# Bias table written later, openings with their token sums and row inside the blocks, and the closing attention's fillers laid out anew

## The chip, the core and the metric

The kernel runs on one core of a Trainium2 chip, as one launch. The metric is the device time of that launch in microseconds (us). Before the change it is 2303.39 us, the median of three runs that lie between 2301.87 and 2303.82 us.

## The reference, cut to what matters

Two transformer blocks are computed one after the other for a sequence of T = 256 tokens, width D = 2048, all in float32.

```python
def first_block(x, c, ...):
    sh1, sc1, g1, sh2, sc2, g2 = split(silu(c) @ w_mod + b_mod, 6)
    h = rms_norm(x, norm_attn) * (1 + sc1) + sh1
    qa, ka, va, qb, ckv, qi, ki, wi = split(h @ w_in)
    out_a = swa_attention(qa, ka, va, attn_sinks, rel_a)       # window 128, bias by bucketed distance
    out_b = dsa_attention(qb, rms_norm(ckv), w_uk, w_uv, qi, ki, wi, rel_b)   # top-64 keys, bias too
    x = x + g1 * (concat(out_a, out_b) @ w_out)
    h = rms_norm(x, norm_ffn) * (1 + sc2) + sh2
    x = x + g2 * conv_ffn(h, w_up, conv_w, conv_b, w_down)
    return rms_norm(x, norm_final)

def second_block(x, c, ...):
    x = x + gA * gmlp_mixer(rms_norm(x) * (1 + scA) + shA, ...)
    k_nope, k_rope, v = mla_shared_kv(rms_norm(x, kv_norm) * (1 + kvsc) + kvsh, ...)
    x = x + gB * mla_mixer(rms_norm(x) * (1 + scB) + shB, k_nope, k_rope, v, ...)   # 16 heads, causal
```

The bias of both attentions of the first block comes from one table: `rel_bias` (32 buckets x 32 heads) spread over 384 distances.

## The kernel before, in words

**Products.** Every weight is streamed from memory once: SyncE's queue (SP) starts the loads, 1 MB each into one of five buffers `raw` (`load`, L323). ScalarE (ACT) rounds a half of a block to its high part `wh` (L331), VectorE (DVE) forms the rest `wl` (L332), each in five buffers, and TensorE (PE) forms the product from three matmuls for each 128 x 128 piece (L342 to L344): high x high, high x low, low x high. A block of 2048 x 128 weights is two halves of 8 pieces, 48 matmuls in all. The results stand in eight PSUM banks, taken in turn.

**Order.** The program is written out in Python in one order; a scheduler turns it into a fixed sequence for each engine at build time, by its own model of readiness, and an instruction that comes later in the program may stand ahead of an earlier one that it holds not to be ready. On the chip each engine's sequence, and SP's, is worked off as it stands: an instruction that waits holds up those behind it.

**Beside the products** run 200 reductions on DVE over 1 MB pieces of the modulation weights (`mod_part`, L453 and L456) and some matmuls for the same purpose (`mod_cols`, L469 to L480).

**First attention, k-tiles.** The input projection goes tile by tile over the 16 pieces of the contraction: `tile_of(k)` loads `w_a[k]` (808 KB) and adds 13 products of three matmuls (L737 to L739) to seven banks that stay in use for the whole loop. The loop runs over eight pairs q of such tiles; between them the columns of `sc1` for the next pair are formed with the one bank left. After pair q == 5 comes `tables`: it loads five small constants, multiplies `rel_bias` by a one-hot matrix (L704), adds the mask on DVE (L706), and writes the sum, 32 x 384 numbers, to DRAM (`bias`, L708, on SP). The attention reads it from there much later (`attend`).

**Openings.** The feed-forward part, the gMLP and the last mixer (`mla`) each begin with `opening`. RMS norm needs the sum of squares over all features, which is complete only when the last block of x is. So the first blocks are multiplied with unnormalized pieces `xg`, and `finish` scales their results by R afterwards. Meanwhile `token_sums` (two matmuls with a column of ones, L307, per tile of squares) give the sums, `rsqrt` takes some 12 small DVE instructions (L271 to L285), `diagonal` two more (L293), and `row` spreads the root over the partitions by a matmul (L299). After `row`, `modulated` forms the normalized pieces xs (L521, L529, L262, L263), which later blocks use. Before the change the sums stand after block 0, the row after block 1.

**Last mixer.** After the opening come four blocks `w_bin[0..3]` (the raw queries). Between them stand `norm_root(raw_c)` after block 0, `normed(raw_c)` (the normalized latent `ck`) after block 1, and `norm_root(kr)` after block 2. Then follow gate blocks (`gate`, 16 of them, 48 matmuls each), which are needed late and serve as fillers: `fill(n)` puts n of them where the program would otherwise have only short, dependent steps. Then the attention over eight pairs of heads g: `weights` (scores and softmax), the queries of the next pair, fillers, keys and values of the next four heads, transposes (`outputs`, L605), and products with the values. From g == 4 on the fillers are the eight blocks of the first half of the output projection.

Of the kernel before, what the change touches and what calls it, by code (L numbers as in the profile page):

```python
# [37 lines left out]

WOB = (0, 2)

NPRE, NMID, NF, NG = 3, 2, 6, 5

RP, RWA, RWB, RF, RG, RM = 1.8, 1.25, 1.25, 0.82, 0.5, 0.6

# [158 lines left out]
class Build:  # L203
# [159 lines left out]
    def opening(self, src, n, sums, roots, rest):  # L363

        w = [self.weights(src(i), DB, 0) for i in range(NPRE)]
        out = [self.multiplied(w[0], self.xg, 2)]
        diag = self.diagonal(roots(sums()))
        out += [self.multiplied(w[i], self.xg, 2) for i in range(1, NMID)]
        R = self.row(diag)
        out += [self.multiplied(w[i], self.xg, 2) for i in range(NMID, NPRE)]  # L370
        with self.tc.issue_after(self.chain):
            rest(0, R)
            for i in range(NPRE, n):
                out.append(self.block(src(i), self.xg, 0, 2))
                rest(i - 2, R)
        return out, R
# [317 lines left out]
    def tables(self, pool):  # L694
        nc = self.nc
        self.causal = pool.tile([P, 384], F32, name="causal")
        nc.sync.dma_start(self.causal, self.ap["causal"])
        self.sinks = pool.tile([P, 16], F32, name="sinks")
        nc.sync.dma_start(self.sinks, self.ap["sinks"].to_broadcast((P, 16)))
        onehot, bneg, rel = (self.tmp("pT", (32, n)) for n in (384, 384, 32))  # L700
        for t, n in ((onehot, "onehot"), (bneg, "bneg"), (rel, "rel_bias")):
            nc.sync.dma_start(t, self.ap[n])
        ps = self.bank()
        nc.tensor.matmul(ps[:32, :384], rel, onehot, start=True, stop=True)  # L704
        bt = self.tmp("pT", (32, 384))
        nc.vector.tensor_add(bt, ps[:32, :384], bneg)  # L706
        self.bias = self.dr.tile([32, 384], F32, name="bias")
        nc.sync.dma_start(self.bias, bt)  # L708

    def first_attention(self):  # L710
        nc, ap = self.nc, self.ap
        with self.tc.tile_pool(name="pa", bufs=1, reuse_waits="tile") as pool:
# [5 lines left out]
            def modulated(blocks):  # L718
                s = slice(blocks[0], blocks[-1] + 1)
                nc.vector.scalar_tensor_tensor(gain[:, s], self.mod_tile("sc1")[:, s], 1.0,  # L720
                                               self.vec("norm_attn", blocks[0], len(blocks)), op0=OP.add, op1=OP.mult)
                xs.extend(self.modulated(self.R, gain, self.mod_tile("sh1"), blocks))
# [3 lines left out]
            def tile_of(k):  # L726

                raw = self.load(ap["w_a"][k], WA)
                x = xs[k]
                hl = [self.parts(raw, 0, 1024), self.parts(raw, 1024, WA)]  # L730
                for i in (12, *range(12)):
                    h, l = hl[i // 8]
                    n = 80 if i == 12 else P
                    s = slice(i % 8 * P, i % 8 * P + n)
                    ps = sums[i // 2][:n, i % 2 * T:i % 2 * T + T]
                    mm = nc.tensor.matmul
                    mm(ps, h[:, s], x[:, :T], start=k == 0 and i % 2 == 0, stop=False)  # L737
                    mm(ps, h[:, s], x[:, LO:], start=False, stop=False)  # L738
                    mm(ps, l[:, s], x[:, :T], start=False, stop=k == DB - 1 and (i % 2 == 1 or i == 12))  # L739

            modulated(range(2))
            for q in range(8):
                if q < 7:
                    a = self.mod_cols("sc1", q + 1)
                    next(a)
                    self.mod_part("sh1", 2 * q + 2)
                tile_of(2 * q)
                if q < 7:
                    next(a)
                    next(a, None)  # L750
                    self.mod_part("sh1", 2 * q + 3)
                    modulated(range(2 * q + 2, 2 * q + 4))
                tile_of(2 * q + 1)
                if q == 5:
                    self.tables(pool)

            keys = self.pair()
            kiT = keys[:, 0]
# [343 lines left out]
    def mla(self):  # L1102
        nc, ap = self.nc, self.ap
        mm = nc.tensor.matmul
        rate = RM
        with self.tc.tile_pool(name="pm", bufs=1, reuse_waits="tile") as pool:
# [15 lines left out]
            raw_q = [two[i // 2][:, i % 2] for i in range(4)]  # L1122
            for i in range(4):
                self.evac(raw_q[i], self.block(ap["w_bin"][i], xs, rate)[:, :T])
                if i == 0:
                    root_c = self.norm_root(raw_c, 512)
                if i == 1:
                    ck = self.normed(raw_c, root_c, self.vec("kva", 0, 4))
                if i == 2:
                    root_k = self.norm_root([kr[:64]], 64)  # L1130

            zs = {}
# [7 lines left out]
            def fill(n):  # L1140
                for _ in range(n):
                    next(more, None)
# [25 lines left out]
            krT = pool.tile([P, T], F32, name="krT")  # L1168
            nc.vector.tensor_add(krT, t1, kn)

            cq = self.normed(raw_q, root_q, self.vec("gqa", 0, 4))
            cs = self.tmp("t", (P, 2, 64))
            nc.sync.dma_start(cs.rearrange("p a b -> p (a b)"), ap["cs"])
            g = self.tmp("t", (P, 64))
# [9 lines left out]
            def keys(c4):  # L1184

                banks = self.token_block([ap["w_ukv"][c4]], ck, 512, rate)
                rn = self.head_roots(lambda tb: banks[tb], 4, P)
                kk = self.wp.tile([P, 2, 4, P], F32, name="kk", tag="c_all", bufs=1)
                for tb in range(2):
                    nc.vector.tensor_mul(kk[:, tb], banks[tb].rearrange("p (a b) -> p a b", a=4),  # L1190
                                         rn[:, tb * 4:tb * 4 + 4].unsqueeze(2).to_broadcast([P, 4, P]))
                yield
                kT = [self.pair(), self.pair()]
                for tb in range(2):
                    ps = self.bank()
                    for h in range(4):
                        nc.tensor.transpose(ps[:, h * P:(h + 1) * P], kk[:, tb, h], self.ident)
                    for half in range(2):
                        nc.scalar.activation(kT[half][:, :, tb * P:(tb + 1) * P], _two(ps[:, half * T:half * T + T]),
                                             AF.Copy, scale=self.vec("gkn"))  # L1200
                yield kT

            def values(c4):
                banks = self.token_block([ap["w_ukv"][4 + c4]], ck, 512, rate)
                vv = [self.pair(), self.pair()]
                for tb in range(2):
                    for half in range(2):
                        self.evac(vv[half][:, tb], banks[tb][:, half * T:half * T + T])
                return vv
# [68 lines left out]
            def outputs(g, s, vv):  # L1278
                pTs = [self.transposed(s[:, r]) for r in range(2)]
                yield  # L1280
                ys = []
                for r in range(2):
                    ps = self.bank()[:, :T]
                    self.values(ps, pTs[r], vv[:, 0, r * P:(r + 1) * P], vv[:, 1, r * P:(r + 1) * P])
                    y = self.tmp()
                    nc.vector.tensor_mul(y, ps, zs[g][:, r])
                    ys.append(self.split(y))
                yield ys
# [8 lines left out]
            def projects():  # L1297
                for b2 in range(8):
                    project(0, b2, ys, gB)
                    yield  # L1300
# [6 lines left out]
            vv = values(0)  # L1307
            fill(1)
            kT = next(k1)
            q = next(q1)  # L1310
            for g in range(8):
                if g == 4:
                    more = projects()
                s = weights(*q, kT[g])
                o = outputs(g, s, vv[g])
                if g < 7:
                    q1 = queries(g + 1)
                    next(q1)
                fill(2 if g < 4 else 1)
                if g % 2 == 1 and g < 7:  # L1320
                    k1 = keys(g // 2 + 1)
                    next(k1)
                    vv += values(g // 2 + 1)
                else:
                    fill(1)
                next(o)
                if g < 4 or g == 5:
                    fill(1)
                if g < 7:
                    if g % 2 == 1:  # L1330
                        kT += next(k1)
                    q = next(q1)
                (ys if g < 4 else ys2).extend(next(o))
# [34 lines left out]
```

## Time and profile before

| what | value |
|---|---|
| median of three runs | 2303.39 us |
| the profiled execution's own time | 2303.12 us |
| its span, first to last instruction | 2301.4 us |
| TensorE busy | 2241.6 us, 97% of the span |
| VectorE busy | 1830.5 us, 80% |
| ScalarE busy | 1157.8 us, 50% |
| mean data rate | 274 GB/s |

The span is 1.7 us shorter than the execution's own time. TensorE's busy time overlaps from one matmul to the next, so 97% does not say that the array works at its peak; the time in which TensorE has nothing at all to run is the 59.8 us that are missing to the span, and the slow clock comes on top where it has been idle for a while.

### The profile page before, as it was taken

How to read it: one execution, taken by the hardware profiler on the slowest of the kernel's cores; microseconds unless marked ns; L12 is line 12 of the kernel's file. 1: busy time of each engine (PE TensorE's matmuls, PEld its weight loads, DVE VectorE, ACT ScalarE, POOL GpSimd, SP SyncE). 2: the span in 40 equal slices, each digit the busy share in tenths (PEclk: the TensorE clock that was granted, in tenths of full speed). 3: DMA queues.
4: the chain of work that ended last, by engine and by line, in shares of the span. 5: the costliest groups of instructions: out<-in, count | busy, mean ns of one | idle time of the engine just before them, and what ended most of it. 6: DMA issues, size and time to landing. Idle time of an engine off the chain costs nothing.

```text
span 2301.4 us, 43110 instructions
## 1 busy us (share of the span) xinstructions
PE 2241.6 (97%) x17710; PEld 2137.8 (93%) x17710; DVE 1830.5 (80%) x2996; ACT 1157.8 (50%) x1918; POOL 4.0 (0%) x8
## 2 busy tenths in 40 slices
PE   6889999999999999999999999999999999999999
PEld 4778889999999999999998889999999999899899
DVE  5768988998898898888798769777776568766784
ACT  2346675664354444444675444435344456555652
POOL 0000000000000000000000000000000000000000
PEclk9999999999999999999999999999999999999999
DMA  8988998898898999899677776887775555444442
GB/s 342 410 334 316 342 350 317 299 323 323 327 375 319 337 361 341 304 366 335 206 252 282 282 276 246 292 284 275 279 273 187 186 187 180 143 155 156 138 147 92
DMA packets 98199, 629.61 MB, mean 274 GB/s; under 512 B 10994, under 2 KB 18130, under 8 KB 30802
## 3 DMA queue, kind: packets, MB, share of 16 engines
q1 hardware_dynamic: 98002, 626.87, 74.5%
q8 instruction: 138, 2.26, 0.4%
q14 instruction: 59, 0.48, 0.1%
HBM read 624.68 MB, written 2.15 MB: 272 GB/s over the span
## 4 chain that ended last, share of the span: by engine, by line
PE 89%; DVE 5%; ACT 2%; DMA 2%; issue 1%; SPq 0%; DVEq 0%; ACTq 0%
PE bank L342 23%; PE bank L343 23%; PE bank L344 23%; PE bank L408 4%; PE bank L409 4%; PE bank L410 4%; DVE wl L332 2%; PE bank L739 1%; PE bank L737 1%; DVE mraw L456 1%; PE bank L738 1%; PE bank L469 1%; DMA mraw<-in_wmods_dram 1%; ACT wh L331 1%; PE bank L1054 1%
## 5 line engine op out<-in xcount | busy, mean ns | idle before, releaser
L342 PE MATMUL bank<-act,wh 128*128 128x256 f32 (+1 forms) x4800 | 1357.4, 283 | 6.2 <-ACT act L549 2.6
L343 PE MATMUL bank<-act,wh 128*128 128x256 f32 x4800 | 1352.1, 282 | 0.2
L344 PE MATMUL bank<-act,wl 128*128 128x256 f32 (+1 forms) x4800 | 1346.6, 281 | 2.3 <-DVE wl L332 2.3
L331 ACT ACTIVATE wh<-raw 128x1024 fp32r<-128x1024 f32 (+3 forms) x770 | 766.2, 1002 | 708.3 <-PE bank L343 489.4
L332 DVE TENSOR_TENSOR wl<-raw,wh 128x1024 fp32r<-128x1024 f32 (+3 forms) x770 | 879.1, 1151 | 208.4 <-ACT wh L331 201.7
L342 PEld LDWEIGHTS bank<-act,wh 128*128 128x128 f32 x4800 | 907.8, 189 | 13.8 <-issue 4.4
L344 PEld LDWEIGHTS bank<-act,wl 128*128 128x128 f32 x4800 | 906.2, 189 | 3.2 <-DVE wl L332 2.9
L343 PEld LDWEIGHTS bank<-act,wh 128*128 128x128 f32 x4800 | 906.7, 189 | 1.0 <-DVE act L263 0.7
L456 DVE CUSTOM_DVE_ANT_0 mraw<-mraw,c_all,k_vecs 128x2048 f32<-128x2048 f32 x200 | 469.3, 2347 | 67.4 <-DMA mraw<-in_wmods_dram 63.3
L408 PE MATMUL bank<-wh,act 128*128 128x512 f32 (+1 forms) x392 | 151.9, 387 | 0.0
L409 PE MATMUL bank<-wl,act 128*128 128x512 f32 (+1 forms) x392 | 151.2, 386 | 0.0
L410 PE MATMUL bank<-wh,act 128*128 128x512 f32 (+1 forms) x392 | 150.9, 385 | 0.0
L262 ACT ACTIVATE act<-t 128x256 fp32r<-128x256 f32 x166 | 66.2, 414 | 95.2 <-DVE t L951 47.7
L408 PEld LDWEIGHTS bank<-wh,act 128*128 128x128 f32 x392 | 73.6, 188 | 15.7 <-PE bank L1258 1.0
L410 PEld LDWEIGHTS bank<-wh,act 128*128 128x128 f32 x392 | 73.6, 188 | 15.2 <-issue 0.7
L409 PEld LDWEIGHTS bank<-wl,act 128*128 128x128 f32 x392 | 73.6, 188 | 14.9 <-issue 0.7
L263 DVE TENSOR_TENSOR act<-t,act 128x256 fp32r<-128x256 f32 x166 | 67.6, 424 | 17.1 <-ACT act L262 16.3
L737 PE MATMUL bank<-act,wh 128*128 128x256 f32 (+1 forms) x208 | 59.7, 301 | 11.7 <-ACT wh L331 11.6
L738 PE MATMUL bank<-act,wh 128*128 128x256 f32 (+1 forms) x208 | 58.3, 294 | 0.0
L739 PE MATMUL bank<-act,wl 128*128 128x256 f32 (+1 forms) x208 | 54.2, 299 | 3.8 <-DVE wl L332 3.8
L737 PEld LDWEIGHTS bank<-act,wh 128*128 128x128 f32 (+1 forms) x208 | 40.8, 198 | 16.4 <-ACT wh L331 14.8
L578 DVE SCALAR_TENSOR_TENSOR X<-bank,m_g,X 128x256 f32<-128x256 f32 x96 | 46.0, 481 | 6.8 <-PE bank L344 4.8
(236 smaller groups left out, 1368.0 us busy)
## 6 DMA issues: line engine op xcount, KB each, us to landing
mraw<-in_wmods_dram SPq DMA_DIRECT2D x200, 1024.0 KB, 6.9
raw<-in_w_up_dram SPq DMA_DIRECT2D x88, 1024.0 KB, 6.4
raw<-in_w_down_dram SPq DMA_DIRECT2D x64, 704.0 KB, 5.5
raw<-in_w_u_dram SPq DMA_DIRECT2D x32, 1024.0 KB, 5.2
raw<-in_w_v_dram SPq DMA_DIRECT2D x32, 1024.0 KB, 4.9
raw<-in_w_z_dram SPq DMA_DIRECT2D x32, 1024.0 KB, 4.9
raw<-in_w_ao_dram SPq DMA_DIRECT2D x32, 1024.0 KB, 5.0
raw<-in_w_cols_dram SPq DMA_DIRECT2D x24, 1024.0 KB, 7.9
```

The lines of the kernel that those rows point to most:

```text
L331: nc.scalar.activation(h[:, :n], raw[:, lo:hi], AF.Copy)
L332: nc.vector.tensor_sub(l[:, :n], raw[:, lo:hi], h[:, :n].bitcast(F32))
L342: mm(ps[:, :n], h[:, s], x[:, :n], start=first and k == 0, stop=False)
L343: mm(ps[:, :T], h[:, s], x[:, LO:], start=False, stop=False)
L344: mm(ps[:, :n], l[:, s], x[:, :n], start=False, stop=last and k == len(xs) - 1)
L408: mm(ps, xh, h[:, s], start=k == 0, stop=False)
L409: mm(ps, xh, l[:, s], start=False, stop=False)
L410: mm(ps, xl, h[:, s], start=False, stop=k == kt - 1)
L456: self.nc.vector.tensor_tensor_reduce(out=raw, in0=raw, in1=self.c_all, scale=1.0, scalar=self.vec("b_" + name, j), op0=OP.mult, op1=OP.ad ...
L737: mm(ps, h[:, s], x[:, :T], start=k == 0 and i % 2 == 0, stop=False)
L738: mm(ps, h[:, s], x[:, LO:], start=False, stop=False)
L739: mm(ps, l[:, s], x[:, :T], start=False, stop=k == DB - 1 and (i % 2 == 1 or i == 12))
```

## The change

It does the following. `tables` is called after pair q == 4 instead of q == 5 and no longer writes the table to DRAM; the new method `table_out` does that, after pair q == 6. `opening` puts the token sums, the root and its diagonal between the two halves of block 0, and the row between the two halves of block 1. In `mla` the two roots and the normalized latent move one block later each; one filler goes ahead of the normalized queries, one ahead of the transposed queries of the first pair; and g = 0, 1 and 2 get one filler instead of two behind `weights`.

```diff
-NPRE, NMID, NF, NG = 3, 2, 6, 5
+NPRE, NF, NG = 3, 6, 5
 
     def opening(self, src, n, sums, roots, rest):
 
         w = [self.weights(src(i), DB, 0) for i in range(NPRE)]
-        out = [self.multiplied(w[0], self.xg, 2)]
+        out = [self.bank() for _ in range(2)]
+        self.product(out[0], w[0][0], self.xg[:8], True, False, ext=2)
         diag = self.diagonal(roots(sums()))
-        out += [self.multiplied(w[i], self.xg, 2) for i in range(1, NMID)]
+        self.product(out[0], w[0][1], self.xg[8:], False, True, ext=2)
+        self.product(out[1], w[1][0], self.xg[:8], True, False, ext=2)
         R = self.row(diag)
-        out += [self.multiplied(w[i], self.xg, 2) for i in range(NMID, NPRE)]
+        self.product(out[1], w[1][1], self.xg[8:], False, True, ext=2)
+        out += [self.multiplied(w[i], self.xg, 2) for i in range(2, NPRE)]
         with self.tc.issue_after(self.chain):
...
         bt = self.tmp("pT", (32, 384))
         nc.vector.tensor_add(bt, ps[:32, :384], bneg)
+        return bt
+
+    def table_out(self, bt):
         self.bias = self.dr.tile([32, 384], F32, name="bias")
-        nc.sync.dma_start(self.bias, bt)
+        self.nc.sync.dma_start(self.bias, bt)
...
                 tile_of(2 * q + 1)
-                if q == 5:
-                    self.tables(pool)
+                if q == 4:
+                    bt = self.tables(pool)
+                if q == 6:
+                    self.table_out(bt)
...
             for i in range(4):
                 self.evac(raw_q[i], self.block(ap["w_bin"][i], xs, rate)[:, :T])
-                if i == 0:
+                if i == 1:
                     root_c = self.norm_root(raw_c, 512)
-                if i == 1:
+                if i == 2:
                     ck = self.normed(raw_c, root_c, self.vec("kva", 0, 4))
-                if i == 2:
+                if i == 3:
                     root_k = self.norm_root([kr[:64]], 64)
...
             nc.vector.tensor_add(krT, t1, kn)
 
+            fill(1)
             cq = self.normed(raw_q, root_q, self.vec("gqa", 0, 4))
...
             vv = values(0)
             fill(1)
             kT = next(k1)
+            fill(1)
             q = next(q1)
             for g in range(8):
...
                 if g < 7:
                     q1 = queries(g + 1)
                     next(q1)
-                fill(2 if g < 4 else 1)
+                fill(2 if g == 3 else 1)
```

## Rows read from the trace of the kernel before

**Rows 1.** Windows by stage: busy us and count per engine, granted clock, DMA share, GB/s.

```profile
421.00:1177.00 756.00, 751.22 (x6345) 750.55 (x6346) 665.33 (x851) 377.20 (x561) 1.59 (x2) 1.00 0.88 322
1177.00:1919.00 742.00, 741.96 (x5546) 707.34 (x5545) 556.42 (x744) 347.27 (x459) 2.16 (x2) 1.00 0.71 252
1919.00:2018.00 99.00, 92.21 (x685) 88.38 (x684) 79.07 (x220) 57.99 (x103) 0.00 (x0) 0.97 0.47 158
2018.00:2253.00 235.00, 230.60 (x1671) 214.48 (x1670) 173.47 (x530) 135.25 (x275) 0.00 (x0) 1.00 0.44 151
```

**Rows 2.** SP's queue in time: start us, us of issuing, transfer; k-tile stage.

```profile
2.96 0.43 SPq L697 DMA_DIRECT2D causal<-in_causal_dram  x1
...
99.88 0.33 SPq L323 DMA_DIRECT2D raw<-in_w_a_dram  x1
...
108.53 0.42 SPq L702 DMA_DIRECT2D pT<-in_rel_bias_dram  x1
...
118.31 0.33 SPq L708 DMA_DIRECT2D bias<-pT  x1
118.73 0.38 SPq L323 DMA_DIRECT2D raw<-in_w_a_dram  x1
```

**Rows 3.** SP's waits, 110 to 120 us: us in total, times, longest.

```profile
SPq L708 <- DVE pT L706: 8.1, 1, 8.1
```

**Rows 4.** Timeline of the k-tile stage: start, us, instruction, [idle before <- releaser].

```profile
100.31 0.61 PE L478 MATMUL bank<-ones,t 128*128 128x1 f32 x4 [0.49 <-ACT t L474]
...
114.39 0.61 PE L478 MATMUL bank<-ones,t 128*128 128x1 f32 x4 [0.49 <-ACT t L474]
...
126.04 0.58 PE L737 MATMUL bank<-act,wh 128*128 128x256 f32 x1 [3.98 <-ACT wh L331]
...
135.09 0.61 PE L478 MATMUL bank<-ones,t 128*128 128x1 f32 x4 [0.49 <-ACT t L474]
```

**Rows 5.** Windows of 2 us in the k-tile stage, columns as in rows 1.

```profile
118.00:120.00 2.00, 2.00 (x19) 2.00 (x19) 2.00 (x3) 0.00 (x0) 0.00 (x0) 1.00 0.31 50
...
126.00:128.00 2.00, 1.96 (x8) 1.84 (x9) 1.91 (x2) 0.57 (x1) 0.00 (x0) 0.50 1.00 420
```

**Rows 6.** Timeline of the three openings (feed-forward, gMLP, last mixer).

```profile
464.60 0.51 PE L342 MATMUL bank<-act,wh 128*128 128x256 f32 x2 [0.74 <-ACT act L262]
...
1180.29 0.42 DVE L317 TENSOR_TENSOR nacc<-nacc,t 128x256 f32<-128x256 f32 x1
...
1182.43 0.50 PE L307 MATMUL bank<-ones,ssacc 128*128 128x1 f32 x4
...
1954.06 0.38 PE L342 MATMUL bank<-act,wh 128*128 128x256 f32 x1 [0.55 <-ACT act L262]
...
1956.28 0.39 PE L342 MATMUL bank<-act,wh 128*128 128x256 f32 x1 [0.90 <-ACT act L262]
```

**Rows 7.** Timeline of the last mixer behind its opening.

```profile
1960.76 0.99 PE L307 MATMUL bank<-ones,nacc 128*128 128x1 f32 x4 [3.52 <-DVE nacc L317]
...
1981.80 0.47 DVE L293 TENSOR_SCALAR t<-k_ident,rs_y 128x128 f32<-128x128 f32 x2
...
1987.28 0.68 PE L299 MATMUL bank<-t,ones 128*128 128x256 f32 x2
...
1995.74 0.67 PE L299 MATMUL bank<-t,ones 128*128 128x256 f32 x2 [1.67 <-DVE t L293]
...
2020.52 0.49 PE L1250 MATMUL bank<-pair 128*128 128x128 f32 x2 [1.37 <-ACT pair L1240]
...
2028.74 1.01 DVE L1275 TENSOR_SCALAR s<-s,b_r 128x128 f32<-128x128 f32 x4
...
2044.79 0.82 PE L605 MATMUL bank<-k_ident,s 128*128 128x128 f32 x6
...
2156.08 1.23 PE L1197 MATMUL bank<-k_ident,kk 128*128 128x128 f32 x8 [0.70 <-DVE kk L1190]
```

**Rows 8.** Window of 2 us behind the first stall of rows 7.

```profile
1962.00:1964.00 2.00, 2.00 (x11) 2.00 (x11) 1.83 (x7) 0.20 (x1) 0.00 (x0) 0.50 0.03 8
```

## The prediction

> **What bounds the kernel now.** I read the windows by stage first, to see where TensorE lacks work. In the feed-forward part it is busy 751.22 of 756 us, in the gMLP 741.96 of 742 [rows 1]. There is nothing to win there but instructions, and the change takes none away: it only moves steps. The prologue of the last mixer is different (92.21 of 99 us), and so is its attention (230.60 of 235) [rows 1]. From the feed-forward row comes the price of a matmul: 751.22 us / 6345 = 0.1184 us, so a block of 48 costs 5.68 us and a half 2.84 us. Then I looked through the timeline of TensorE for idle time in brackets, and for each such place through what it waited on. Five places belong to lines that the diff touches: 3.98 us in the k-tile stage [rows 4], 3.52, 1.67, 1.37 and 0.70 us in the last mixer [rows 7], and three small ones at the ends of openings [rows 6]. Everything else in the kernel has no part in the sum; the forecast is the price of these places.
>
> **The table write.** SP works off its sequence in order. It reached the write of the table 8.1 us before it could issue it, since DVE had not yet added the mask [rows 3]; it issued it at 118.31 and the next `w_a` load at 118.73 [rows 2]. The pair before had its `w_a` load at 99.88, and a usual pair lasts 114.39 - 100.31 = 14.08 us [rows 4]; so the load was due at 113.96 and went 4.77 us late. Meanwhile the transfers ran dry: a DMA share of 0.31 and 50 GB/s in 118 to 120 us [rows 5]. TensorE then stood idle for 3.98 us [rows 4], and afterwards ran at the lower of its two levels: granted clock 0.50, 8 matmuls in 2 us where it had done 19 [rows 5]. The pair took 135.09 - 114.39 = 20.70 us, 6.62 more than a usual one [rows 4]: 3.98 idle, and 2.64 for the slow stretch.
>
> After the change the table is computed about one pair, 14 us, earlier, and the write stands at least two `w_a` loads later. By then its data are there, so the write costs SP one issue, 0.33 us, and its loads wait for buffers anyway; that wait hides it, and without it the loads would go 0.33 us later. `rel_bias` is loaded a pair earlier too (0.42 us on SP, at its place in the program today) [rows 2]; the other constants already went out at the start, as `causal` at 2.96 did [rows 2]. The small matmul and the DVE addition fall into the pair before; I have no usual pair that contains them, so I bound them by 0 and by the 0.99 us of the dearest four small matmuls [rows 7] and take 0.3. The gain is 6.62 - 0.3 = 6.3 us. It is 6.62 at most; at least the idle 3.98 less 0.99, if the clock falls for another reason all the same.
>
> The Trainium skill ("TensorE: Matmul & The Clock Gate", section "What's actually happening") says that the number of slow matmuls in a cold stretch varies from run to run, and advises not to fit it. By that only the idle time would count: 3.98 - 0.3 = 3.7 us here.
>
> **The openings.** Sums and row both move half a block, 2.84 us, earlier, and their distance stays one block. So the normalized pieces begin up to 2.84 us earlier, which covers the three waits for them: 0.74 us in the feed-forward opening, 0.55 and 0.90 in the last mixer's [rows 6]. I count all of it, 2.19 (least 0, if DVE, and not the row, sets their pace). In the gMLP there is no idle time to win. What can be late now are the sums' inputs. In the gMLP the sums started at 1182.43 and would start at 1179.59; the last addition to the second accumulator ends at 1180.29 + 0.42 = 1180.71 [rows 6]: TensorE may wait 1.1 us, or nothing where matmuls of the second half are put ahead. I take 0.5 there and 0.3 for the last mixer (same bounds), 0 for the feed-forward part. The small DVE instructions of the root move ahead of `wl` halves, which are formed up to five ahead; that lead hides them, and without it a stall like the 0.74 would come of it. Sum: 2.19 - 0.8 = 1.4 us won (2.2 at most; 2.2 lost at worst).
>
> **The last mixer.** TensorE waited 3.52 us for the squares of the latent [rows 7]. Now block 1, 5.68 us, stands there, more than the wait. Behind the wait the clock was at 0.50: 11 matmuls in 2 us instead of 17 [rows 8], that is 0.7 us lost in that window, and the four small matmuls took 0.99 instead of 0.50 [rows 6, 7], 0.49 more. So the slow stretch cost at least 1.2 and, by the pair above, up to 2.64; I take 1.9. Gain 5.4 us (4.7 to 6.2). What is late next: the root of the rope key, now behind block 3. Its diagonal was done at 1981.80 + 0.47 = 1982.27 and used at 1987.28 [rows 7]; of that 5.01 us a block takes 5.68, so 0 to 0.7 are lost; I take 0.3.
>
> The filler ahead of the normalized queries covers the 1.67 us with 5.68. The filler ahead of the first pair's transposed queries lets DVE catch up, but the step from transposes over ScalarE to the scores stays; of 1.37 us [rows 7] I count 0.7 (0 to 1.37). The fillers also come out differently: before, 17 places asked for 16 gates, and the last place of g = 3 found none, so that the keys' transposes waited 0.70 us [rows 7]; after it there are 5 + 3 + 2 + 3 + 3 = 16 places, and a gate stands there: 0.7 won. Pairs g = 0 to 2 lose one filler each ahead of their transposes. For g = 0 the softmax was done at 2028.74 + 1.01 = 2029.75, and the transposes began at 2044.79 [rows 7]: of 15.04 us of cover 5.68 go and 9.4 stay, so it costs nothing; beyond 15 it would cost what is missing. For the shorter lead of the next queries I take 0.3 (0 to 1.37). Sum: 5.4 - 0.3 + 1.67 + 0.7 + 0.7 - 0.3 = 7.9 us won (at most 9.9).
>
> **Sum.** 6.3 + 1.4 + 7.9 = 15.6 us. Against the profiled execution's own 2303.12 (span 2301.4 and 1.7 around it) that is 2287.5. The median of the runs is 0.3 above that execution, which is nothing beside the terms.
>
> **The rivals.** *The write keeps its place.* The sequence for SP is made by readiness: `causal`, which the program loads after pair q = 5, went out at 2.96 us. If the write is put forward the same way, to where its data are just not ready, SP stands again. Against it: `rel_bias` went out at 108.53 [rows 2], right where the program has it, behind the load of k-tile 11, so SP's sequence here mostly follows the program. Then only 9.3 us are won: 2293.8. *The last mixer gives half.* The moved roots and fillers meet other work on DVE, and waits come back in other places; 4.0 instead of 7.9: 2291.4. *The clock gives nothing back*, because another short wait lets it fall: 2.64 and 1.9 us go out of the sum: 2292.0. The rows speak against it, as both slow stretches stand right behind the idle times in question. The advice of the Trainium skill ("TensorE: Matmul & The Clock Gate", section "What's actually happening") would give this sum. *The gain is returned.* The new sequence puts other transfers that depend on late work ahead of loads; each costs what the write cost, 6.62, and two make 13.2: 2300.7. Nothing shown speaks for it; it can't be excluded, since a build orders everything anew. *Slower.* TensorE takes its matmuls in order, so sums that are not ready hold up the second half of the block. The place is the L307 inside block 0 of the three openings; the price is the lateness of the accumulators plus a slow stretch of 2.64 where the idle time is as long as 3.98. It decides once the three together exceed 15.6 + 4.6 us, 6.7 each, that is 4.1 us late and a slow stretch; the rows show 1.1. Say 7 each: 2308.5 with the small terms.
>
> The Trainium skill ("PSUM — Partial Sum Buffer", section "Engine vs sequencer instructions") says that matmuls start and complete in program order, which is the rule behind this last rival; the trace agrees, as nothing ran in the 3.52 us ahead of an L307.
>
> **How the numbers follow.** Forecast 0.56, the write keeps its place 0.12, half in the last mixer 0.14, no clock gain 0.05, returned 0.08, slower 0.05. About 0.2%, 4.6 us, is what a measurement of this kernel can tell from no change. Faster by more: 0.56 + 0.12 + 0.14 + 0.05 = 0.87; within: 0.08; slower: 0.05. The range: with every term at its best (6.62 + 2.19 + 9.9 = 18.7) the time is 2284.4, and a rebuilt order may remove one more stall of the size of 3.5 elsewhere: 2281. At the other end the first two rivals together leave 1.4 + 4.0: 2297.7, taken as 2298. Beyond it lie the returned gain and the slower case.
>
> **What would show it.** In the k-tile stage all pairs last about 14 us, the write waits for nothing, and the clock stays at 1.00 from 120 to 135 us. In the last mixer no wait above 1 us stands before an L307 or L299, and the clock stays up. At g = 3 the wait of the keys' transposes is gone. The gMLP's opening may show up to 1.1 us of new idle time at L307. The forecast is wrong if SP again waits for L706, if new idle time of several us shows in stages that the diff does not touch, or if the waits of the last mixer reappear one step later.

## The result, and the profile after

| | before | after |
|---|---|---|
| median of 4 runs each | 2303.61 us (2301.87 to 2305.90) | 2291.07 us (2287.94 to 2292.16) |
| profiled execution | 2303.12 us, span 2301.4 | 2291.75 us, span 2290.0 |

The ratio is 0.9942, with a 95% interval of 0.993 to 0.9954. The kernel is 12.5 us faster; 15.6 were forecast, and 2291.07 lies inside 2281 to 2298.

SP's queue after the change, in time (start us, us of issuing, transfer):

```profile
97.46 0.42 SPq L705 DMA_DIRECT2D pT<-in_rel_bias_dram  x1
...
126.76 0.33 SPq L323 DMA_DIRECT2D raw<-in_w_a_dram  x1
127.14 0.84 SPq L714 DMA_DIRECT2D bias<-pT  x1
128.03 0.91 SPq L323 DMA_DIRECT2D raw<-in_w_a_dram  x2
```

The write (now L714) goes out right behind a `w_a` load, and SP's waits from 90 to 135 us name neither it nor its table; the 8.1 us of [rows 3] are gone. Its issue took 0.84 us, where the prediction had counted 0.33. The pairs of k-tiles in TensorE's timeline, one row at the end of each (L478 is now L481):

```profile
57.65 0.61 PE L481 MATMUL bank<-ones,t 128*128 128x1 f32 x4 [0.49 <-ACT t L477]
...
73.54 0.61 PE L481 MATMUL bank<-ones,t 128*128 128x1 f32 x4 [0.49 <-ACT t L477]
...
117.30 0.61 PE L481 MATMUL bank<-ones,t 128*128 128x1 f32 x4 [0.49 <-ACT t L477]
...
133.00 0.61 PE L481 MATMUL bank<-ones,t 128*128 128x1 f32 x4 [0.49 <-ACT t L477]
```

The long pair is gone: 133.00 - 117.30 = 15.70 us, where it was 20.70 [rows 4]. But a pair that nothing in the change touches, 57.65 to 73.54, took 15.89 us, and the usual pair of [rows 4] took 14.08. So something other than the write can lengthen a pair by as much as 1.8 us here.

The last mixer in the timeline after the change:

```profile
1958.28 0.50 PE L307 MATMUL bank<-ones,nacc 128*128 128x1 f32 x4
...
1964.39 0.59 PE L299 MATMUL bank<-t,ones 128*128 128x256 f32 x2
...
1989.59 0.59 PE L299 MATMUL bank<-t,ones 128*128 128x256 f32 x2
...
2019.48 0.71 PE L1259 MATMUL bank<-pair 128*128 128x128 f32 x4 [1.06 <-ACT pair L1249]
...
2130.59 0.40 PE L413 MATMUL bank<-wh,act 128*128 128x512 f32 x1
...
2137.94 1.08 ACT L1106 ACTIVATE sq<-bank 128x512 f32<-128x512 f32 x2
...
2144.77 1.32 PE L1206 MATMUL bank<-k_ident,kk 128*128 128x128 f32 x8 [1.86 <-DVE kk L1199]
```

No bracket stands behind the L307 (1958.28) and the L299 (1989.59) that waited 3.52 and 1.67 us [rows 7], nor behind the L299 of the rope key (1977.28), for which the prediction had put down 0.3. The first scores wait 1.06 instead of 1.37 us. One wait grew: the key transposes at g = 3 (L1197, now L1206) waited 0.70 us and were forecast to wait for nothing; they wait 1.86. The last matmul of the keys' block ended at 2130.59 + 0.40, yet their squares (`sq`), from which the root for the keys is formed, began only at 2137.94.

### The profile page after: what moved, and what is told of

Same layout as the page of the kernel before. It is cut to its first block, busy times and chain, and to the rows that moved or that the text cites. A ratio compares the mean times of both kernels' runs of the same rounds, so it can differ in the third digit from the quotient of the medians.

```text
span 2290.0 us, 43088 instructions
## 1 busy us (share of the span) xinstructions
PE 2241.9 (98%) x17710; PEld 2138.7 (93%) x17710; DVE 1828.7 (80%) x2996; ACT 1156.7 (51%) x1918; POOL 7.6 (0%) x8
## 4 chain that ended last, share of the span: by engine, by line
PE 92%; DVE 4%; ACT 1%; DMA 1%; issue 1%; SPq 0%; ACTq 0%; DVEq 0%
PE bank L342 24%; PE bank L343 24%; PE bank L344 24%; PE bank L412 4%; PE bank L411 4%; PE bank L413 4%; DVE wl L332 1%; DVE mraw L459 1%; PE bank L745 1%; PE bank L743 1%; PE bank L472 1%; PE bank L744 1%; DMA raw<-in_w_a_dram 1%; ACT wh L331 1%; PE bank L608 1%
## 5 line engine op out<-in xcount | busy, mean ns | idle before, releaser
L342 PE MATMUL bank<-act,wh 128*128 128x256 f32 (+1 forms) x4800 | 1359.1, 283 | 4.1 <-ACT act L552 2.6
L344 PE MATMUL bank<-act,wl 128*128 128x256 f32 (+1 forms) x4800 | 1347.2, 281 | 1.4 <-DVE wl L332 1.4
L342 PEld LDWEIGHTS bank<-act,wh 128*128 128x128 f32 x4800 | 907.7, 189 | 11.0 <-issue 5.5
L344 PEld LDWEIGHTS bank<-act,wl 128*128 128x128 f32 x4800 | 905.7, 189 | 2.1 <-DVE wl L332 1.8
L413 PE MATMUL bank<-wh,act 128*128 128x512 f32 (+1 forms) x392 | 151.1, 385 | 0.0
L413 PEld LDWEIGHTS bank<-wh,act 128*128 128x128 f32 x392 | 73.6, 188 | 14.8 <-issue 0.3
L948 ACT ACTIVATE t<-bank,k_vecs 128x256 f32<-128x256 f32 x41 | 23.0, 561 | 61.8 <-PE bank L344 61.8
```

The source lines that it names most:

```text
L342: mm(ps[:, :n], h[:, s], x[:, :n], start=first and k == 0, stop=False)
L344: mm(ps[:, :n], l[:, s], x[:, :n], start=False, stop=last and k == len(xs) - 1)
L413: mm(ps, xl, h[:, s], start=False, stop=k == kt - 1)
```

## The experiments

In the expectations, theory A is the sum of the prediction; theory B is what the two traces suggested beside it. A ratio is that to the kernel before, measured beside it, with its 95% interval; the microseconds are worked out from it and the median of before (2303.6 to 2304.6).

### The four parts, each alone

Each of the four kernels is the kernel before with one part of the change's diff.

e1_table:
```diff
+        return bt
+    def table_out(self, bt):
...
-                if q == 5:
-                    self.tables(pool)
+                if q == 4:
+                    bt = self.tables(pool)
+                if q == 6:
+                    self.table_out(bt)
```

> The kernel before with the later bias write alone (its tables made two pairs of k-tiles later). Theory A, the terms of the prediction: the pair that carries the write loses its excess, 14.1 us for a pair instead of 20.7, so the run is 6.3 us shorter. Theory B, read from the two traces: the pairs of this stage are paced by the landing of their loads, whose rate differs from one execution to the next (the pair that starts at 57.65 us took 15.89 in the changed kernel and 14.07 in the kernel before, ahead of anything that the change moves); then the long pair goes, but over many executions the gain is only 2 to 4 us.

(By the edit the table is made one pair earlier and only written one pair later than before.)

e2_opening: only the `opening` part of the diff (sums and row between the halves of the blocks).

> The kernel before with the token sums and the row between the halves of the opening blocks, alone. Theory A: the waits for xs at the openings of the gMLP-FFN and of the last mixer go (0.74, 0.55 and 0.90 us), the opening of the gMLP block loses up to 0.5, in all 1.4 us shorter. Theory B: as A in the trace; the wait for the last mixer's root stays near 3.5 us, and the time is within 0.1% of the kernel before.

e3_roots: only `root_c`, `ck` and `root_k`, each one block of `w_bin` later.

> The kernel before with the last mixer's root and normalised tiles between its projections, alone. Theory A: the wait of 3.52 us and the 1.9 us of slow clock behind it go, 0.3 us comes back at the key's root: 5.1 us shorter. Theory B: the same here, 4 to 7 us shorter, since nothing in this stage waits for a transfer; this and the fillers carry most of what the whole change gains.

e4_fillers:
```diff
+            fill(1)
             cq = self.normed(raw_q, root_q, self.vec("gqa", 0, 4))
...
             kT = next(k1)
+            fill(1)
...
-                fill(2 if g < 4 else 1)
+                fill(2 if g == 3 else 1)
```

> The kernel before with the fillers of the closing attention spread anew, alone. Theory A: the waits of 1.67 us (cq) and 0.70 us (q) go and so does 0.70 at the last group's key transposes, less 0.3: 2.8 us shorter. Theory B, read from the changed kernel's trace: the first two go, but at the last group's key transposes the wait grows from 0.70 to about 1.85 us, since the slots of the token tiles stay taken until the last gate, so the gain is 1 to 1.5 us.

| part | A | ratio | shorter by |
|---|---|---|---|
| table | 6.3 | 0.9991 (0.9981 to 1.0002) | 2.1 us (-0.5 to 4.4) |
| openings | 1.4 | 0.9989 (0.9981 to 0.9998) | 2.5 us (0.5 to 4.4) |
| roots | 5.1 | 0.9973 (0.9962 to 0.9983) | 6.2 us (3.9 to 8.8) |
| fillers | 2.8 | 1.0002 (0.9993 to 1.0010) | -0.5 us (-2.3 to 1.6) |

They sum to 10.3 us; the four intervals are too wide to tell this from 12.5. The openings and the roots do what A said. For the fillers A's 2.8 lies outside the interval, and theory B's 1 to 1.5 inside it; of 6.3 for the table at most 4.4 is left. In e1_table's timeline the pair in question is short all the same:

```profile
116.67 0.61 PE L478 MATMUL bank<-ones,t 128*128 128x1 f32 x4 [0.49 <-ACT t L474]
...
131.65 0.61 PE L478 MATMUL bank<-ones,t 128*128 128x1 f32 x4 [0.49 <-ACT t L474]
```

14.98 us. So the gain is made there, and part of it seems to be lost elsewhere. In e3_roots the latent's squares are no longer late, and the waits of 0.55 and 0.90 us at the end of the opening [rows 6] are gone too, though the opening is unchanged; but the latent's row is late:

```profile
1962.80 0.61 PE L307 MATMUL bank<-ones,nacc 128*128 128x1 f32 x4
...
1970.69 0.67 PE L299 MATMUL bank<-t,ones 128*128 128x256 f32 x2 [1.50 <-DVE t L293]
```

The 1.50 us are missing in the changed kernel, most likely because the opening there makes its tiles earlier; the two parts were not tried together alone. In e4_fillers the 1.67 us ahead of `cq` are gone and the first scores wait 1.06 instead of 1.37 us, but the g = 3 transposes wait the same 1.86 us as in the changed kernel, 1.16 more than before: of 2.0 us won in waits more than half was given back here.

```profile
2161.10 1.31 PE L1198 MATMUL bank<-k_ident,kk 128*128 128x128 f32 x8 [1.86 <-DVE kk L1191]
```

### The table undone in the changed kernel, the changed kernel again, and a write one pair later

e5_undo_table, against the changed kernel:
```diff
-                if q == 4:
+                if q == 5:
                     bt = self.tables(pool)
-                if q == 6:
                     self.table_out(bt)
```

e7_write_later changes only `q == 4` to `q == 5` and keeps the write at `q == 6`; e6_after_again is the changed kernel itself.

> The changed kernel with the bias table made and written where it was in the kernel before; the openings, the roots and the fillers stay changed. Theory A: the pair of k-tiles that carries the write is about 20 us long again and the run is 6.3 us longer than the changed kernel (about 0.997 of the kernel before). Theory B: the pair is that long again, but what it costs is given back in part where TensorE is back to back: in 1600 to 1750 us the kernels with the table left alone issued 1278 matmuls, the two with the table moved 1273 and 1274; this one issues 1278 and is only 2 to 4 us longer than the changed kernel (about 0.9955).

> The changed kernel once more, a second profiled execution and more times. Both theories: 12.5 us shorter than the kernel before, 0.993 to 0.9955. Theory B1 (the slower pace belongs to the program, through the order in which the tables' tiles take their slots): 1272 to 1275 matmuls in 1600 to 1750 us again. Theory B2 (it belongs to the execution): any number from 1272 to 1279. Of the pairs of k-tiles: if the transfers' pace belongs to the execution, other lengths than 15.89, 14.02, 15.76, 13.98 and 15.70 us, between 14.0 and 16.4.

> The changed kernel with the table made at the pair where the kernel before makes it, and only its write left in its later place, one pair behind. Theory A: SyncE's write finds its table done or nearly so (the table was added up 8 us after the write's first place, a pair lasts 14), no long pair, the time of the changed kernel within 0.1%. Theory B1: as A for the pair, and the tiles take their slots in the order of the kernel before, so that 1278 matmuls stand in 1600 to 1750 us and the run is 2 to 3 us shorter than the changed kernel. Theory B2: the pace as it falls out, the time of the changed kernel.

Ratios: e5_undo_table 0.9955 (0.9943 to 0.9967), e6_after_again 0.9945 (0.9930 to 0.9959), e7_write_later 0.9942 (0.9929 to 0.9956). With the table undone the long pair is back:

```profile
115.89 0.60 PE L481 MATMUL bank<-ones,t 128*128 128x1 f32 x4 [0.49 <-ACT t L477]
...
135.91 0.61 PE L481 MATMUL bank<-ones,t 128*128 128x1 f32 x4 [0.49 <-ACT t L477]
```

20.02 us. Over all kernels run, this pair took 18.75 to 21.42 us in the five with the write in its old place (mean 20.26) and 13.98 to 15.96 in the eight with the moved write and whole loads (mean 14.79): 5.5 us. Yet e5_undo_table is only 2.3 us slower than e6_after_again by their ratios, whose intervals overlap. What is lost lies in a stretch without idle time. Two matmuls that are the same in all kernels, the last of L344 on 128x258 in the feed-forward opening and in the last mixer's, in the changed kernel and in e5_undo_table:

```profile
456.87 0.28 PE L344 MATMUL bank<-act,wl 128*128 128x258 f32 x1
...
1946.68 0.28 PE L344 MATMUL bank<-act,wl 128*128 128x258 f32 x1
```

```profile
460.11 0.28 PE L344 MATMUL bank<-act,wl 128*128 128x258 f32 x1
...
1947.42 0.28 PE L344 MATMUL bank<-act,wl 128*128 128x258 f32 x1
```

1489.81 us against 1487.31: the later write costs 2.50 us between them, in which no wait of TensorE is longer than 0.1 us. The other six kernels with both the later write and the changed openings, e12_places (below) left aside, took 1489.74 to 1490.21, and e2_opening, which has the old write and the changed openings, 1487.30. The first of the two matmuls itself stands at 455.7 us in the mean of seven kernels with the later write and at 461.1 in the five with the old one, so the 5.4 us won in the k-tile stage are still there when the stretch begins. Windows by stage show the same: in 1600 to 1750 us the kernels with the old place issued 1278 matmuls, those with the new one 1273 or 1274, e6_after_again and e7_write_later (1274 both) among them. So it belongs to the program (B1 or a like reason), not to the execution. The clause of B1 that e7_write_later would issue 1278 is refuted: making the table in its old place does not help. From the end of the k-tile stage on, every tile of e7_write_later lies where it lies in the changed kernel, so what moves the tiles is the later write and not the making of the table.

The pairs of e6_after_again took 15.54, 15.30, 14.90, 15.48 and 14.06 us, those of the first execution 15.89, 14.02, 15.76, 13.98 and 15.70: the length of one and the same pair varies from execution to execution.

### The gate at g = 3

e8_fill3, against the changed kernel:
```diff
-                fill(2 if g == 3 else 1)
+                fill(3 if g == 3 else 1)
...
-                if g < 4 or g == 5:
+                if g < 3 or g == 5:
                     fill(1)
```

> The changed kernel with the sixteenth gate issued with two others ahead of the last group's keys, and none behind them. Theory A (the gate behind is a cover): without it the last group's key transposes wait longer than the 1.85 us of the changed kernel, by up to the gate's 5.9. Theory B (the gate behind keeps the token tiles alive and so the squares of the keys start 7 us late): the squares start as the keys' block ends and the wait is 0.70 us as in the kernel before; about 1 us shorter than the changed kernel, within the uncertainty of the time.

```profile
2133.64 1.30 ACT L1106 ACTIVATE sq<-bank 128x512 f32<-128x512 f32 x2 [1.26 <-PE bank L413]
...
2141.13 1.31 PE L1206 MATMUL bank<-k_ident,kk 128*128 128x128 f32 x8 [0.58 <-DVE kk L1199]
```

Theory B: the squares now wait for the keys' block itself (L413) and no longer start 7 us after it; the transposes wait 0.58 us instead of 1.86. (The keys of g = 3, "the last group's" in the expectation, are the third of four groups.) The ratio is 0.9926 (0.9914 to 0.9939), with 2288.26 us the fastest of the kernels that do all the work; its interval overlaps that of e6_after_again, so in the whole time a gain is not shown. It is in the traces: from the last L344 on 128x258 to the end of the span e8_fill3 took 342.1 us and e10_best, which has the same edit, 342.2; five kernels with the gate behind the keys (the changed kernel, e6_after_again, e7_write_later, e9_banks, e12_places) took 343.3 to 343.6.

The slots are the reason. In the program of the changed kernel the two tiles of squares take the slots of two token tiles (normalized pieces xs) that the gate behind the keys still reads, and the first of them waits for this matmul of the gate:

```profile
2137.66 0.28 PE L344 MATMUL bank<-act,wl 128*128 128x256 f32 x1
```

It ends at 2137.94, where the squares begin. In e8_fill3 and in the kernel before the gates that read these tiles come before the keys, and the squares wait for L413 (L410 before).

### Where the matmuls lose 2.5 us

From the last stage of the first attention on, e5_undo_table and the kernels with the later write have the same instructions in the same order on every engine; what differs is where tiles lie: the eight PSUM banks are numbered otherwise, two pairs of token-tile slots in SBUF are exchanged, and three of the five load buffers.

e9_banks, against the changed kernel (e10_best has it together with the edit of e8_fill3):
```diff
+        d = [self.bank() for _ in range(8)]
+        for i in [*range(8), 2, 6, 5, 7, 1, 4, 3, 0]:
+            nc.vector.memset(d[i][:1, :1], 0.0)
+        nc.vector.memset(self.bank()[:1, :1], 0.0)
```

> The changed kernel with another numbering of its PSUM banks and nothing else: at the very start each of the eight banks is written twice in one column by VectorE and one of them a third time, which lets the banks come free in another order, so that from the first attention on every matmul writes the bank that it writes in the kernel with the table undone; the order of the instructions on every engine is that of the changed kernel. Theory B1 (the slower pace of the kernels with the later write comes from which PSUM banks their products fall into): 1278 matmuls in 1600 to 1750 us and 3195 in 800 to 1177 us, as in the kernels with the table in its old place, and 2 to 2.5 us shorter than the changed kernel. Rival B3 (it comes from the two pairs of token-tile slots that differ too): 1274 and 3190, the time of the changed kernel.

> The changed kernel with both mends: the sixteenth gate ahead of the last group's keys, and the numbering of the PSUM banks. Theory B1: the gains add, 1 us and 2 to 2.5 us, so about 2288 us beside 2291.5 of the changed kernel and 2304 of the kernel before (0.9925). Rival B3: only the gate's, about 2290 us.

e12_places does the same for the token-tile slots, the load buffers and the banks at once.

> The changed kernel with the places of all its tiles of SBUF and PSUM renumbered, by tiny writes of VectorE into every slot at the very start, so that from the first attention on every instruction of every engine reads and writes the addresses that it has in the kernel with the table undone (which issued 3195 matmuls in 800 to 1177 us and 1278 in 1600 to 1750 us); the order of the instructions on each engine stays that of the changed kernel. The first loads wait for these writes, so the start is some 5 to 10 us later and the time of the whole says little. Theory B3 (the slower pace comes from the places in SBUF; the banks alone did nothing): 3195 and 1278. Rival B5 (it comes from neither, but from something that no row shows, such as the code's own place or its semaphores): 3189 or 3190, and 1273 or 1274, as in the six kernels with the later write.

The same two matmuls in e9_banks and in e12_places:

```profile
454.09 0.28 PE L348 MATMUL bank<-act,wl 128*128 128x258 f32 x1
...
1943.83 0.28 PE L348 MATMUL bank<-act,wl 128*128 128x258 f32 x1
```

```profile
458.35 0.28 PE L356 MATMUL bank<-act,wl 128*128 128x258 f32 x1
...
1945.65 0.28 PE L356 MATMUL bank<-act,wl 128*128 128x258 f32 x1
```

1489.74 and 1487.30 us. And the windows of 1600 to 1750 us (busy us and count per engine, granted clock, DMA share, GB/s), of e9_banks and of e12_places:

```profile
1600.00:1750.00 150.00, 150.00 (x1273) 150.00 (x1273) 109.21 (x134) 64.20 (x79) 0.00 (x0) 1.00 0.73 261
```

```profile
1600.00:1750.00 150.00, 150.00 (x1279) 150.00 (x1278) 110.11 (x136) 64.37 (x79) 0.00 (x0) 1.00 0.73 262
```

The banks alone change nothing: B1 as put there is refuted. All places at once give the 2.5 us back to within 0.01: B3 against B5. In 800 to 1177 us e12_places issued 3193 matmuls and not 3195; but it reaches the sums of the gMLP's opening inside this window, and up to 1150 us it issued 2967, as e5_undo_table did, against 2963 in the changed kernel and in e9_banks. TensorE is busy throughout and its granted clock is 1.00 in both; over 150 to 350 us TensorE gets through 0.1 to 0.3% fewer matmuls with the one set of places. Which of the SBUF tiles it is, token tiles or load buffers, or whether they need the banks beside them, stays open, and so does the reason. e9_banks took 0.9939 (0.9925 to 0.9953), the time of the changed kernel, and e10_best 0.9936 (0.9925 to 0.9948), 2290.0 us, both as B3 has it; e12_places took 2291.75 us in its one run, with a start 2 us later, where 5 to 10 were expected.

The Trainium skill ("SBUF — State Buffer", section "SBUF: two separate sides") says that TensorE, ScalarE and VectorE's own ports to SBUF never wait on anyone. That gives no reason why places should cost anything; the runs show 2.5 us in 1490 between two placings, and the measurement decides. No run shows whether a port is what it is about.

### Lighter loads in the k-tile stage

e11_light, against the changed kernel; it leaves out the product over the second half of these loads:
```diff
+        h = D // 2 if name == "sh1" else D
-        self.nc.sync.dma_start(raw, self.ap["wmods"][i, j])
+        self.nc.sync.dma_start(raw[:, :h], self.ap["wmods"][i, j][:, :h])
```

> The changed kernel with half of each load of the shift sh1 in the stage of the first k-tiles: the product over the second half of its rows is left out, so the loads of a pair are 1 MB lighter and the rest of the work on TensorE is as it was. Theory B (the pairs that take 14.5 to 16.4 us are those that wait for their loads): all five pairs take 14.0 to 14.1 us. Rival (the long ones come from the clock or from the chain of VectorE and ScalarE): one or more of them still takes over 14.5 us.

```profile
53.80 0.61 PE L482 MATMUL bank<-ones,t 128*128 128x1 f32 x4 [0.49 <-ACT t L478]
...
67.64 0.60 PE L482 MATMUL bank<-ones,t 128*128 128x1 f32 x4 [0.49 <-ACT t L478]
...
109.07 0.60 PE L482 MATMUL bank<-ones,t 128*128 128x1 f32 x4 [0.49 <-ACT t L478]
...
122.91 0.60 PE L482 MATMUL bank<-ones,t 128*128 128x1 f32 x4 [0.49 <-ACT t L478]
```

All five pairs take 13.76 to 13.85 us, even less than the 14.0 to 14.1 expected, those with the table's matmul and its write too. The single run took 2281.86 us. The edit also shortens VectorE's reduction of the same tile by half, but the traces speak for the loads. ScalarE's waits (us in total, times, longest) in the first of the five pairs, in the changed kernel and in e11_light:

```profile
ACT wh L331 <- DMA raw<-in_w_a_dram: 5.2, 2, 4.7
```

```profile
ACT wh L331 <- DMA raw<-in_w_a_dram: 0.2, 1, 0.2
```

In the changed kernel ScalarE waited so for `w_a` for 4.2 to 5.2 us in the three pairs of 15.70 to 15.89 us and for 2.9 and 3.0 in the two of 13.98 and 14.02; in e11_light for at most 1.9. So the long pairs wait for their loads. The clock takes part: in two of the three long ones, 15.76 and 15.70, it was 0.89 over the pair, worth 1.7 us; in all five of e11_light it was 1.00.

## Why the prediction was right, and where its terms were off

**The table write: the mechanism right, the size not.** SP no longer waits, the 3.98 us and the 20.70 us pair are gone, and the long pair comes back (20.02) when the part is undone. The term 6.62 was mis-sized in two ways. It was measured against a usual pair of 14.08 us, nearly the shortest there is; against the mean of executions the long pair cost 5.5 us. And its cost of 0.3 left out what a changed sequence does to the rest of the kernel: 2.5 us in matmuls that run back to back from other places in SBUF. 5.5 - 2.5 is 3.0 us; measured alone were 2.1 (-0.5 to 4.4). The 0.3 itself, for the small matmul and the addition, was not measured by itself. Of the rival "the gain is returned" a part came true, by no mechanism that was named: no transfer was put ahead of a load.

**The openings: right.** The three waits of 2.19 us [rows 6] are gone. The 0.5 us put against the gMLP did not come: no wait of a matmul over 0.1 us stands at its opening. A matmul of the block (L342, at 1176.38) was put ahead of the second sum, which started at 1176.71, and its accumulator was done at 1176.20. So the part is worth its upper bound, 2.2; measured were 2.5 (0.5 to 4.4).

**The last mixer: right as a sum.** From the last L344 on 128x258 (1948.61 before, 1946.68 after) to the end of the span, the stretch shrank from 352.8 to 343.3 us, 9.5 us. The prediction's terms for it are 7.9 and the opening's 0.55 + 0.90 - 0.3, together 9.05. That they agree so well is in part luck: TensorE's idle time in the stretch fell by 6.2 us (14.5 to 8.3), where these terms put 7.1, and the rest, 3.3 for 1.9, is time in which the same 2487 matmuls now run faster.

Within it, the wait of 3.52 us and the slow clock behind it are gone: in e3_roots alone 6.2 us (3.9 to 8.8) for 5.1. The prediction had read the slow stretch from one execution. From the L307 behind this wait to the next L299 on 128x256, 52 matmuls, the kernel before took 8.03 us (from 1960.76 [rows 7]) and e2_opening 9.28:

```profile
1968.79 0.59 PE L299 MATMUL bank<-t,ones 128*128 128x256 f32 x2
```

```profile
1957.61 0.98 PE L307 MATMUL bank<-ones,nacc 128*128 128x1 f32 x4 [3.52 <-DVE nacc L317]
...
1966.89 0.59 PE L299 MATMUL bank<-t,ones 128*128 128x256 f32 x2
```

The changed kernel takes 1964.39 - 1958.28 = 6.11 us for 52 of the same kinds, with no wait ahead of them. So the slow stretch cost 1.9 us in the one, as the prediction took it, and 3.2 in the other behind the same wait (e4_fillers 3.2, and 2.9 in e1_table behind 3.23 us). With their mean, 2.8, wait and slow stretch make 6.3, near the 6.2 measured; the 1.45 us won at the opening and the 1.50 lost at the row cancel.

The step that failed is the last filler. "After it a gate stands there: 0.7 won" took the gate as a cover for the key transposes; it stands there, but the squares that the transposes depend on lie in slots that this gate still reads, they begin 7 us after the keys, and the wait grew by 1.2 us. It can cost more: behind the same 1.86 us the granted clock from 2145 to 2150 us was 0.68 in e5_undo_table and 1.00 in the changed kernel, and from these transposes to the last wait of 0.80 us (L616) e5_undo_table took 96.84 us and the changed kernel 95.16. The fillers alone gave -0.5 us (-2.3 to 1.6) for 2.8.

**The clock.** The prediction gave 2.64 and 1.9 us to slow stretches behind two waits. Behind the moved root no window of the changed kernel from 1950 to 1975 us is under 1.00. In the k-tile stage the clock did not stay up from 120 to 135 us, as it had said it would: behind a wait of 0.95 us for `wh` (118.85) it was 0.66.

```profile
120.00:125.00 5.00, 4.84 (x28) 4.77 (x28) 4.00 (x6) 1.34 (x4) 0.00 (x0) 0.66 1.01 420
```

So a part of the rival "the clock gives nothing back" came true in this stage and execution. What one and the same wait does to the clock varies. Windows of 5 us, in the changed kernel and in e8_fill3, around two waits of 1.42 and 1.44 us that both have (from 280.48 and from 277.07 us on):

```profile
275.00:280.00 5.00, 4.06 (x35) 3.85 (x33) 5.00 (x6) 1.27 (x4) 0.00 (x0) 1.00 0.68 223
280.00:285.00 5.00, 3.08 (x23) 2.88 (x24) 5.00 (x5) 2.32 (x3) 0.00 (x0) 1.00 0.93 312
```

```profile
275.00:280.00 5.00, 2.14 (x12) 1.73 (x11) 5.00 (x6) 3.22 (x4) 0.00 (x0) 0.79 0.80 274
280.00:285.00 5.00, 5.00 (x27) 5.00 (x25) 3.50 (x4) 0.00 (x0) 0.00 (x0) 0.52 0.86 303
```

No clock is lost in the one, (1 - 0.79 + 1 - 0.52) x 5 = 3.5 us of full speed in the other. The Trainium skill ("TensorE: Matmul & The Clock Gate", section "What's actually happening") says of the slow matmuls at the start of a kernel that their number varies from run to run; these rows show the like in the middle of one. A term for it has to be a mean, and a difference of 2 to 3 us between two single traces shows no gain by itself.

**The sum.** Of the 3.1 us by which the forecast was too fast, the table's term explains about as much (6.3 against 3.0); the fillers' loss (2.8 against about nothing) is made up, as far as the intervals tell, by the roots and the openings. That the time fell into the range says little for the sum: the range is 17 us wide, and 2291.07 lies as near to the sums of two rivals, 2291.4 (half in the last mixer) and 2292.0 (no clock gain). The last mixer gave its whole sum, so the first did not come true, and the second only in the k-tile stage. Of the signs, those on the write and on the waits and the clock of the last mixer came; the pairs of 14 us, the clock from 120 to 135 us and the wait at g = 3 did not.

## What to carry to other kernels

A wait at the head of an in-order queue of transfers is worth what the stage behind it loses on average (here 5.5 us, where one trace showed 6.6); take the usual length of a step from several steps and executions, not from the best ones of one trace. A filler covers a chain only if the chain's start does not need something that the filler still holds, so look at when the first instruction of the chain begins, not only at the work beside it. When a change gains less than its own rows show, measure a fixed pair of instructions across a stage that it does not touch: a slowdown without any idle time is seen only there.

## What the runs showed of the hardware that was not expected

Matmuls that run back to back at granted clock 1.00 took 1489.81 us between two fixed points with one placing of tiles in SBUF and 1487.30 with another, the instructions and their order being the same; the numbering of the PSUM banks made no difference (1489.74). The pairs of k-tiles of one and the same program took 13.98 to 15.89 us in one execution and 14.06 to 15.54 in the next, the second pair 14.02 and 15.30, and with 1 MB less to load per pair 13.76 to 13.85. Behind one and the same wait of 3.52 us, 52 matmuls took 8.03, 9.28 and 9.35 us in three traces, and 52 of the same kinds 6.11 without the wait.
